# A written order for the matrix engine in the expert stage, and the embedding's weight as one more piece of the expert weights

## The chip, the cores and the metric

The kernel runs on one core of a Trainium2 chip, in one launch. The metric is device time in microseconds (us). Before the change the median of three runs is 1607.17 us (1605.23 to 1608.93). The engines are named as the profile names them: PE is the matrix engine, PEld its weight loads, DVE the vector engine, ACT the scalar engine, POOL the GpSimd engine, and SP the engine that here does little but issue DMAs; SPq is its instruction queue.

## What is computed

Two transformer layers follow each other on 256 tokens of width 1024, all in float32. The first mixes attention and a gated delta rule. The second ends in a mixture of 32 experts, and this is where the change lies:

```python
logits = jnp.dot(xt, w_router) + b_router
top_logit, top_e = lax.top_k(logits, 4)
gate = jax.nn.softmax(top_logit, axis=-1)
...
hh = jnp.dot(xs, w_gu[e]) + b_gu[e]              # 1024 x 2048 per expert
glu, lin = jnp.split(hh, 2, axis=-1)
act = jnp.minimum(glu, 7) * sigmoid(1.702 * glu) * (jnp.clip(lin, -7, 7) + 1.0)
return jnp.dot(act, w_dn[e]) + b_dn[e]           # 1024 x 1024 per expert
...
h = h + moe(rmsnorm_2(h, g_moe), ...)
u = rmsnorm_2(h, g_ple)
h = h + sigmoid(u @ w_ple_gate) * (p @ w_ple_proj)   # the embedding: p is 256 x 256
return rmsnorm_2(h, g_final)
```

The weights of the 32 experts are 12 MiB each, 384 MiB together, and each is read once.

## The kernel before

The expert stage takes most of the time, from about 600 to 1566 us. Each expert has 64 rows for its tokens. Experts go through `run` in 17 units: unit 0 is a single expert, unit 8 is one expert with 128 rows (a "double"), and the other fifteen are pairs of experts.

**The stream of weights.** `pieces` yields the weights in the order in which they are used, cut into pieces of 1 MiB (128 partitions x 2048): the gate/up weights of unit i (16 pieces for a pair), then the down weights of unit i-1 (8 pieces). `load` (line 110) issues a DMA for each from SP's queue into the next of 15 buffers, which are taken in turn and carry the names raw (3 and 4 of them), whi and wlo (4 each). A DMA can start when the piece that lay in its buffer 15 pieces earlier has been used by PE. `refill` in `run` asks for further pieces until all buffers but one are taken; `nxt` hands the next one to the matrix instructions.

**One turn of the loop.** For turn i, `run` writes: the gate/up products of unit i (64 matrix instructions of a pair into four PSUM tiles `ph`); the copies of these into `hs` by ACT and DVE; the down products of unit i-1 (32 instructions into two PSUM tiles of the pool `pm`); and then, in `flush`, what is left over, which this text calls **the rest of the turn**: `gather` for unit i+2 (16 matrix instructions, line 1325), the turning of `hs` and the activation of unit i (`activation`, 16 transposes, line 298, with the additions of the bias on DVE, line 1372), the selection matrix (`scatter_rows`, 2 transposes), and `combine` for unit i-1 (8 matrix instructions, line 1401). The four PSUM tiles of `pm` are shared by the down products and all of the rest.

**How a pair is multiplied.** A pair's two experts each use 64 of PE's 128 columns, so the instruction for one expert and the one for the other can run side by side. `products` writes them alternately:

```python
for j in js:
    ...
    for i in range(2):
        ...
        T.matmul(o[64 * i:64 * i + 64], x(i, c_), w_[:, zz, sl], start=first, stop=last)
```

The order that `run` writes is not the order in which the engines get the instructions: a scheduler of the framework reorders each engine's instructions by its own estimates. In the trace every float32 matrix instruction of the program shows as two records.

**The embedding.** `load_embed` loads `p` and the 1 MiB of `w_ple_proj` in turn 13, by way of the same 15 buffers, and appends to `held`, on which `refill` keeps one buffer fewer filled. `embed` uses them in turn 14 (line 1619) and leaves the product in `pv` for the end of the kernel.

**The end.** After the last down product come the last `combine`, the norm, the product with `w_ple_gate` (lines 152 to 154) and the output.

Of the kernel before, what the change touches and what calls it, by code (L numbers as in the profile page):

```python
# [66 lines left out]
def tile_net(ctx: ExitStack, tc: tile.TileContext, a: dict, dbg=None):  # L67
# [982 lines left out]
    wgu = a["w_gu_2"].rearrange("o e d f -> (o e d) f")  # L1050
    wdn = a["w_dn_2"].rearrange("o e d f -> (o e d) f")

    def pieces(units):

        for i in range(len(units) + 1):
            if i < len(units):
                rs = [p["row"]() for p in units[i]["places"]]
                for k in range(8):
                    for r in rs:
                        yield wgu[bass.ds(r + k * P, P)], 1, 2 * D, "(k p) n -> p k n"  # L1060
            if i:
                rs = [p["row"]() for p in units[i - 1]["places"]]
                for q in range(4):
                    for r in rs:
                        yield wdn[bass.ds(r + q * 2 * P, 2 * P)], 2, D, "(p k) n -> p k n"

    def ahead_or_none(order):
        for src, kc, m, rows in order:
# [16 lines left out]
    with ExitStack() as c3:  # L1085
# [220 lines left out]
        ph = c3.enter_context(tc.tile_pool(name="ph", bufs=4, space=bass.MemoryType.PSUM))  # L1306
        pm = c3.enter_context(tc.tile_pool(name="pm4", bufs=4, space=bass.MemoryType.PSUM))

        def gather(b):

            vs = [v for v, _ in rows_of(b)]
            nb = len(vs)
            dd = wk.tile([P, 2, 2, 64], F32, name="dd", bufs=1)
            for t in range(2):
                for i in range(nb):
                    V.tensor_scalar(dd[:, t, i], iota, vs[i](t), None, ALU.is_equal)
            b["xs"] = wk.tile([P, 8, P], F32, name="xs", bufs=2)
            n = nb * 64
            yield
            for z in range(2):  # L1320
                ps = pm.tile([P, 4, P], F32, name="pm")
                for c_ in range(4):
                    ds_ = slice((4 * z + c_) * P, (4 * z + c_ + 1) * P)
                    for t in range(2):
                        T.matmul(ps[:, c_, :n], ut[t][:, ds_], dd[:, t, :nb], start=t == 0, stop=t == 1)  # L1325
                A.copy(b["xs"][:, 4 * z:4 * z + 4, :n], ps[:, :, :n])
                yield

        def scatter_rows(b):

            dg = wk.tile([P, 2, 2, 64], F32, name="dg", bufs=1)
            rs = rows_of(b)
            for t in range(2):
                for i, (v, g) in enumerate(rs):
                    n = 3 - len(rs)
                    V.tensor_scalar(dg[:, t, i:i + n], bm(iota, n), v(t), g(t), ALU.is_equal, ALU.mult)
            yield
            ps = pm.tile([P, 2, P], F32, name="pm")
            for t in range(2):
                transpose(ps[:, t], dg[:, t].rearrange("p a s -> p (a s)"))  # L1340
            b["oh"] = wk.tile([P, 2, P], F32R, name="ohT", bufs=3)
            b["gs"] = wk.tile([P, 1], F32, name="gs", bufs=3)
            V.tensor_scalar(b["oh"], ps, 0.0, None, ALU.is_gt)
            V.tensor_reduce(b["gs"], ps.rearrange("p t k -> p (t k)"), AX.X, ALU.add)
            yield

        def activation(b, z):
# [4 lines left out]
            if z < n:  # L1352
                gl = []
                for i in range(2):
                    ps = pm.tile([P, m, 64 * n], F32, name="pm")
                    for c_ in range(m):
                        q, k = (z * m + c_) // 2, c_ % 2
                        h = b["hs"][i][:, q * 2 * P + k:(q + 1) * 2 * P:2]
                        if n == 1:

                            T.matmul(ps[:, c_], h, cc("fold"), start=True, stop=True)
                        else:
                            transpose(ps[:, c_], h)
                    gl.append(ps)
                for i in range(2):
                    ps = gl[i]
# [28 lines left out]
        def combine(b, tiles=(0, 1)):  # L1395
            for t in tiles:
                pss = [pm.tile([P, 512], F32, name="pm") for _ in range(2)]
                for nh in range(2):
                    ns = slice(nh * 512, nh * 512 + 512)
                    for i, y in enumerate(b["y"]):  # L1400
                        T.matmul(pss[nh], b["oh"][:, t], y[:, ns], start=i == 0, stop=i == 1)  # L1401
                for nh in range(2):
                    o = hres[:, t, nh * 512:nh * 512 + 512]
                    V.tensor_tensor(o, o, pss[nh], ALU.add)
                yield

        def bias_of(ev):
            br = wk.tile([P, 512], F32, name="sw", bufs=4)[:8, :2 * P]
            SY.dma_start(br, a["b_gu_2"][0].rearrange("e (q f) -> e q f", f=2 * P)[bass.ds(ev, 1)].rearrange("o q f -> (o q) f"))
            ps = pm.tile([P, 2, 8], F32, name="pm")  # L1410
            for k in range(2):
                transpose(ps[:, k], br[:, k::2])
            bi = wk.tile([P, 16], F32, name="bie")
            V.tensor_copy(bi.rearrange("p (q k) -> p k q", k=2), ps)
            return bi

        def run(units, order, ready, more=None, room=None):
# [1 line left out]

            more = more or {}  # L1420
            n = len(units)
            held = []

            def refill():
                while len(ready) < slots() - 1 - len(held):
                    r = ahead_or_none(order)
                    if r is None:
                        return
                    ready.append(r)
# [7 lines left out]
            def products(kd, outs, chunk, x, ws, z, nchunks, js=(0, 1)):  # L1437
# [3 lines left out]
                for j in js:  # L1441
                    o = outs[j]
                    sl = slice(j * 512, j * 512 + 512)
                    if kd == "double":
                        T.matmul(o, x(None, chunk), ws[0][:, z, sl], start=chunk == 0, stop=chunk == nchunks - 1)
                        continue
                    for i in range(2):
                        if kd == "pair":
# [2 lines left out]
                        else:  # L1451
                            c_ = chunk + i
                            w_, zz = (ws[i], z) if len(ws) == 2 else (ws[0], z + i)
                            first, last = c_ < 2, c_ >= nchunks - 2
                        T.matmul(o[64 * i:64 * i + 64], x(i, c_), w_[:, zz, sl], start=first, stop=last)  # L1455

            todo = []

# [8 lines left out]
                todo.clear()  # L1467

            def after(i):
                todo.extend(f(held) for f in more.get(i, ()))  # L1470

            drain(gather(units[0]))
            after(-1)
            if n > 1:
                start(gather(units[1]))
            flush()
            done = []
            for i in range(n + 1):
                if i < n:
# [12 lines left out]
                    b["hs"] = [wk.tile([P, D], F32, name="hs", bufs=2) for _ in range(2)]  # L1492
                    for j in (0, 2, 1, 3):
                        (V.tensor_copy if j // 2 else A.copy)(b["hs"][j // 2][:, j % 2 * 512:j % 2 * 512 + 512], hp[j])  # L1494
                    if i + 2 < n:
                        start(gather(units[i + 2]))
                    sc = scatter_rows(b)
                    next(sc)
                    todo += [activation(b, 0), sc, activation(b, 1)]
# [21 lines left out]
            flush()  # L1521
            return done[0]

        def load_biases(held):
            bdn.extend(wk.tile([P, 512], F32, name="bdn", bufs=2) for _ in range(2))
            for nh in range(2):
                nc.gpsimd.dma_start(bdn[nh][:NE], a["b_dn_2"][0][:, nh * 512:nh * 512 + 512])
            yield

        def biases(held):  # L1530

            gT = wk.tile([P, 2, P], F32, name="gT")
            ps = pm.tile([P, 2, P], F32, name="pm")
            for t in range(2):
                transpose(ps[:NE, t], gate[:, t])
            V.tensor_copy(gT[:NE], ps[:NE])
            yield
            for nh in range(2):
                for t in range(2):
                    ns = slice(nh * 512, nh * 512 + 512)  # L1540
                    ps = pm.tile([P, 512], F32, name="pm")
                    T.matmul(ps, gT[:NE, t], bdn[nh][:NE], start=True, stop=True)
                    V.tensor_tensor(hres[:, t, ns], hres[:, t, ns], ps, ALU.add)
                    yield

        bdn, nov = [], []

        def blocks(held):
            nov.append(nc.values_load(novi[0:1, 0:1], min_val=0, max_val=NJ))
            yield  # L1550

# [40 lines left out]
        big = raw2, RAW2  # L1592
        pv, emb = [], []

        def load_embed(held):

            held.append(1)
            pt = wk.tile([P, 2, 256], F32, name="bdn", bufs=2)
            nc.gpsimd.dma_start(pt, a["p_2"][0, 0].rearrange("(t p) d -> p t d", p=P))
            emb.extend((load(a["w_ple_proj_2"][0], 2, D), pt))  # L1600
            yield

        def embed(held):

            w_, pt = emb
            ps = pm.tile([P, 2, 2, P], F32, name="pm")
            for t in range(2):
                for k in range(2):
                    transpose(ps[:, k, t], pt[:, t, k * P:(k + 1) * P])
            pT = wk.tile([P, 2, S], F32, name="sw", bufs=4)  # L1610
            V.tensor_copy(pT, ps.rearrange("p k t q -> p k (t q)"))
            w_ = w_[:, :2 * D].rearrange("p (k n) -> p k n", k=2)
            yield
            pv.extend(keep.tile([P, D], F32, name="w4") for _ in range(2))
            for t in range(2):
                for nh in range(2):
                    ps = pm.tile([P, 512], F32, name="pm")
                    for k in range(2):
                        T.matmul(ps, pT[:, k, t * P:(t + 1) * P], w_[:, k, nh * 512:nh * 512 + 512], start=k == 0, stop=k == 1)
                    A.copy(pv[t][:, nh * 512:nh * 512 + 512], ps)  # L1620
                    yield
            held.pop()

        first = [lambda held, g=g: g() for g in (chosen, gates, changes, overflow)]
        last = run(units, order, ready, {-1: first, 2: [load_biases], 3: [biases], 4: [blocks], len(units) - 4: [load_embed], len(units) - 3: [embed]})

        if "h3" in dbg:
            SY.dma_start(dbg["h3"].rearrange("(t p) d -> p t d", p=P), hres)
# [88 lines left out]
```

## Time and profile before

| | before |
|---|---|
| runs, median (lowest to highest) | 1607.17 us (1605.23 to 1608.93) |
| profiled execution, its own time | 1613.31 us |
| its span, first to last instruction | 1611.4 us |
| PE busy | 1544.6 us, 96% of the span |
| DVE, ACT busy | 627.6 us, 420.0 us |
| DMA, mean over the span | 301 GB/s, 484.89 MB |
| PE's granted clock, mean | 0.982 of 2.4 GHz |

The profiled execution is 0.4% above the median of the runs. The busy share of PE is a poor guide here: its records are modelled to overlap, and two instructions that run side by side and two that run one behind the other both count as busy. What is to be read instead is at which distance the starts follow each other, which engine waits for which, and how many GB/s the DMA engines move in each stretch.

### The profile page before, as it was taken

The numbers are of one execution on the slowest core, as the hardware profiler recorded it, in microseconds if no ns is written. First come the engines' busy times: TensorE is split into PE (matmuls) and PEld (weight loads), VectorE is DVE, ScalarE is ACT, GpSimd is POOL, SyncE is SP. The second block draws the span as 40 slices with busy tenths as digits, with TensorE's granted clock in tenths as the row PEclk, the third lists the DMA queues.
The fourth block names the chain that finished last, engine by engine and source line by source line (L and its number), as shares of the span: only waits on it lengthen the run. The fifth ranks groups of instructions, "written<-read, shape, count | busy, mean of one in ns | idle before, by whom it ended". The sixth has DMA issues, their size and how long they took to land. (4 is left out here: it accounts for less than half of the span.)

```text
span 1611.4 us, 20470 instructions
## 1 busy us (share of the span) xinstructions
PE 1544.6 (96%) x8162; PEld 959.1 (60%) x8162; DVE 627.6 (39%) x1183; ACT 420.0 (26%) x648; POOL 27.9 (2%) x39
## 2 busy tenths in 40 slices
PE   6999999999889989999999999999999999999996
PEld 5889899999689865444434444444444444443435
DVE  6867765466656642311212321221231132120336
ACT  4544554354447521100101110110110011010124
POOL 0000000000000000000000000000000000000001
PEclk9999999999989979999999999999999999999998
DMA  6443323345434188999999999989999999998992
GB/s 208 157 133 130 105 85 126 106 151 186 138 109 156 53 340 362 420 420 421 420 419 421 420 420 421 421 346 384 398 420 421 421 420 422 419 420 347 422 373 77
DMA packets 99247, 484.89 MB, mean 301 GB/s; under 512 B 10470, under 2 KB 14060, under 8 KB 49996
## 3 DMA queue, kind: packets, MB, share of 16 engines
q1 hardware_dynamic: 99004, 483.14, 75.5%
q8 instruction: 66, 1.08, 0.3%
q0 software_dynamic: 144, 0.39, 0.1%
q14 instruction: 33, 0.27, 0.0%
HBM read 482.46 MB, written 1.05 MB: 300 GB/s over the span
## 5 line engine op out<-in xcount | busy, mean ns | idle before, releaser
L1455 PE MATMUL ph<-raw,xs 128*64 128x512 f32 x928 | 245.1, 599 | 0.0
L1494 DVE COPY hs<-ph 128x512 f32<-128x512 f32 x34 | 23.5, 692 | 443.3 <-PE ph L1455 417.9
L1455 PE MATMUL ph<-wlo,xs 128*64 128x512 f32 x536 | 189.8, 599 | 0.0
L310 DVE TENSOR_TENSOR wlo<-raw,whi 128x2048 fp32r<-128x2048 f32 (+4 forms) x73 | 158.0, 2166 | 79.0 <-ACT whi L309 78.8
L204 PE MATMUL pm<-w,whi 128*128 128x256 f32 x640 | 183.7, 288 | 3.0 <-ACT w L309 2.1
L1455 PE MATMUL ph<-whi,xs 128*64 128x512 f32 x520 | 185.1, 598 | 0.0
L206 PE MATMUL pm<-w,wlo 128*128 128x256 f32 x640 | 180.3, 283 | 2.7 <-DVE wlo L310 2.7
L205 PE MATMUL pm<-w,whi 128*128 128x256 f32 x640 | 180.8, 283 | 2.0 <-DVE w L310 1.9
L1455 PE MATMUL pm<-raw,act 128*64 128x512 f32 x528 | 176.0, 601 | 0.0
L309 ACT CAST whi<-raw 128x2048 fp32r<-128x2048 f32 (+4 forms) x73 | 131.9, 1808 | 157.0 <-PE pm L205 90.5
L1455 PEld LDWEIGHTS ph<-raw,xs 128*64 128x64 f32 x928 | 88.0, 137 | 126.6 <-issue 126.1
L1494 ACT COPY hs<-ph 128x512 f32<-128x512 f32 x34 | 18.5, 588 | 470.7 <-PE ph L1455 443.6
L204 PEld LDWEIGHTS pm<-w,whi 128*128 128x128 f32 x640 | 122.4, 192 | 3.7 <-ACT w L309 2.4
L206 PEld LDWEIGHTS pm<-w,wlo 128*128 128x128 f32 x640 | 122.4, 192 | 3.1 <-DVE wlo L310 3.1
L205 PEld LDWEIGHTS pm<-w,whi 128*128 128x128 f32 x640 | 122.4, 191 | 2.7 <-DVE w L310 2.6
L1455 PEld LDWEIGHTS ph<-wlo,xs 128*64 128x64 f32 x536 | 58.8, 136 | 75.6 <-issue 75.3
L1455 PEld LDWEIGHTS ph<-whi,xs 128*64 128x64 f32 x520 | 57.9, 136 | 74.7 <-issue 74.7
L1455 PEld LDWEIGHTS pm<-raw,act 128*64 128x64 f32 x528 | 51.7, 136 | 81.8 <-issue 76.9
L1455 PE MATMUL pm<-whi,act 128*64 128x512 f32 x240 | 92.1, 601 | 0.0
L1325 PEld LDWEIGHTS pm<-dd,w 128*128 128x128 f32 x544 | 69.0, 204 | 35.7 <-issue 25.2
L1455 PE MATMUL pm<-wlo,act 128*64 128x512 f32 x224 | 87.2, 602 | 0.0
L1325 PE MATMUL pm<-dd,w 128*128 128x128 f32 (+1 forms) x544 | 77.0, 296 | 1.1 <-issue 1.1
(403 smaller groups left out, 1964.9 us busy)
## 6 DMA issues: line engine op xcount, KB each, us to landing
raw<-in_w_gu_dram SPq DMA_DIRECT2D x116, 1024.0 KB, 14.1
wlo<-in_w_gu_dram SPq DMA_DIRECT2D x71, 1024.0 KB, 16.1
whi<-in_w_gu_dram SPq DMA_DIRECT2D x69, 1024.0 KB, 16.7
raw<-in_w_dn_dram SPq DMA_DIRECT2D x66, 1024.0 KB, 14.4
raw<-in_w_in_dram SPq DMA_DIRECT2D x46, 1024.0 KB, 4.9
whi<-in_w_dn_dram SPq DMA_DIRECT2D x32, 1024.0 KB, 15.2
wlo<-in_w_dn_dram SPq DMA_DIRECT2D x30, 1024.0 KB, 15.4
raw<-in_w_branch_a_dram SPq DMA_DIRECT2D x4, 1024.0 KB
```

What stands on the lines that cost most here:

```text
L204: T.matmul(o, hi[:, k, ns], xh[:, k0 + k], start=first, stop=False)
L205: T.matmul(o, hi[:, k, ns], xl[:, k0 + k], start=False, stop=False)
L206: T.matmul(o, lo[:, k, ns], xh[:, k0 + k], start=False, stop=last)
L309: A.copy(hi, src)
L310: (by or V).tensor_tensor(lo, src, hi.bitcast(F32), ALU.subtract)
L1325: T.matmul(ps[:, c_, :n], ut[t][:, ds_], dd[:, t, :nb], start=t == 0, stop=t == 1)
L1455: T.matmul(o[64 * i:64 * i + 64], x(i, c_), w_[:, zz, sl], start=first, stop=last)
L1494: (V.tensor_copy if j // 2 else A.copy)(b["hs"][j // 2][:, j % 2 * 512:j % 2 * 512 + 512], hp[j])
```

## The change

It does four things. Every matrix instruction and transpose of the expert stage goes through `mm` or `turn_`, which ask the framework to keep them in the order in which they are written. The weight of the embedding becomes one more piece of the stream, behind the pieces that turn 12 uses, and `embed` takes it by `nxt` in turn 12; `p` is loaded in turn 6, and `held` goes. The gather of unit 1, which stood ahead of unit 0's gate/up products, now stands behind them with that of unit 2. And `gather`'s one-hot tile `dd` gets a second buffer.

```diff
+    EMB = 12
...
     def pieces(units):
...
+            if i == EMB:
+                yield a["w_ple_proj_2"][0], 2, D, "(k p) n -> p k n"
...
+        def mm(*x_, **y_):
+
+            return tc.keep_in_program_order(T.matmul(*x_, **y_))
+        def turn_(out, in_):
+            k = in_.shape[0]
+            return tc.keep_in_program_order(T.transpose(out, in_, ident[:k, :k]))
...
-            dd = wk.tile([P, 2, 2, 64], F32, name="dd", bufs=1)
+            dd = wk.tile([P, 2, 2, 64], F32, name="dd", bufs=2)
...
-                        T.matmul(o[64 * i:64 * i + 64], x(i, c_), w_[:, zz, sl], start=first, stop=last)
+                        mm(o[64 * i:64 * i + 64], x(i, c_), w_[:, zz, sl], start=first, stop=last)
...
-                while len(ready) < slots() - 1 - len(held):
+                while len(ready) < slots() - 1:
...
             drain(gather(units[0]))
             after(-1)
-            if n > 1:
-                start(gather(units[1]))
             flush()
...
-                    if i + 2 < n:
-                        start(gather(units[i + 2]))
+                    for u_ in units[i + 2:i + 3] if i else units[1:3]:
+                        start(gather(u_))
...
-            emb.extend((load(a["w_ple_proj_2"][0], 2, D), pt))
...
-            w_, pt = emb
+            pt = emb[0]
+            w_ = nxt()
...
-        last = run(units, order, ready, {-1: first, 2: [load_biases], 3: [biases], 4: [blocks], len(units) - 4: [load_embed], len(units) - 3: [embed]})
+        last = run(units, order, ready, {-1: first, 2: [load_biases], 3: [biases], 4: [blocks], 6: [load_embed], EMB - 1: [embed]})
```

**PE, down products of turn 2, before.** The second two of its eight pieces are raw_6274 (first expert) and raw_6276 (second expert); pm_6375 and pm_6376 are the two halves of the result.

```order
L1455 MATMUL pm_6375<-raw_6274,act_6193 64x512
L1455 MATMUL pm_6376<-raw_6274,act_6193 64x512
L1325 MATMUL pm_6441<-dd_6364,w4_5717 128x128
L1325 MATMUL pm_6441<-dd_6364,w4_5715 128x128
L1325 MATMUL pm_6441<-dd_6364,w4_5717 128x128
L298 MATMUL pm_6451<-C0_66,hs_6358 128x128 x4
L1455 MATMUL pm_6375<-raw_6276,act_6193 64x512
L1455 MATMUL pm_6376<-raw_6276,act_6193 64x512
L1455 MATMUL pm_6375<-raw_6274,act_6193 64x512
L1455 MATMUL pm_6375<-raw_6276,act_6193 64x512
L1455 MATMUL pm_6376<-raw_6274,act_6193 64x512
L1455 MATMUL pm_6376<-raw_6276,act_6193 64x512
```

The same two pieces with the change:

```order
L1316 MATMUL pm_6375<-raw_6274,act_6193 64x512
L1316 MATMUL pm_6375<-raw_6276,act_6193 64x512
L1316 MATMUL pm_6376<-raw_6274,act_6193 64x512
L1316 MATMUL pm_6376<-raw_6276,act_6193 64x512
L1316 MATMUL pm_6375<-raw_6274,act_6193 64x512
L1316 MATMUL pm_6375<-raw_6276,act_6193 64x512
L1316 MATMUL pm_6376<-raw_6274,act_6193 64x512
L1316 MATMUL pm_6376<-raw_6276,act_6193 64x512
```

Four of the eight instructions stood with two of the same expert next to each other and other work around them; now first and second expert alternate throughout, and the gather and the transposes stand behind all 32 down products. (All rows now carry line 1316 or 1320, where `mm` and `turn_` stand.) In turn 5, where PE reads a register, the order is still a mixture of the two.

**PE, start of the stage, before**: the end of unit 0's gather (128x64), unit 0's gate/up (ph) and unit 1's gather (128x128).

```order
L1325 MATMUL pm<-dd,w_5715 128x64
L1325 MATMUL pm<-dd,w_5717 128x64
L1455 MATMUL ph<-raw,xs 64x512
L1325 MATMUL pm<-dd,w_5715 128x128
L1325 MATMUL pm<-dd,w_5717 128x128
```

and with the change:

```order
L1316 MATMUL pm<-dd,w_5715 128x64
L1316 MATMUL pm<-dd,w_5717 128x64
L1316 MATMUL ph<-raw,xs 64x512 x25
L1316 MATMUL ph<-whi,xs 64x512
L1316 MATMUL ph<-raw,xs 64x512
```

Unit 1's sixteen gather instructions have moved behind unit 0's 32 gate/up products, where unit 2's sixteen stand too.

**SP, the load of the embedding's weight.** Before, it stands between gate/up pieces of turn 14:

```order
L110 DMA wlo<-in_w_gu_dram 128x2048
L110 ISA
L110 DMA whi<-in_w_gu_dram 128x2048
L110 DMA whi<-in_w_ple_proj_dram 128x2x1024
L110 ISA
L110 DMA wlo<-in_w_gu_dram 128x2048
```

and with the change behind the last down piece of turn 12:

```order
L110 DMA whi<-in_w_dn_dram 128x2048
L110 ISA
L110 DMA wlo<-in_w_dn_dram 128x2048
L110 DMA wlo<-in_w_ple_proj_dram 128x2x1024
L1086 TENSOR_LOAD eidi
L1086 ISA x2
```

The number of DMAs on SP is the same; the one has moved ahead by 62 pieces of the experts.

## Rows read from the trace of the kernel before

**Rows 1.** SP's queue, waits from 540 to 1580 us: for what, us, times, longest.

```profile
SPq L110 <- PE ph L1455: 301.0, 180, 17.1
SPq L110 <- PE pm L1455: 198.6, 80, 8.8
...
SPq L110 <- PE pm L1619: 20.1, 1, 20.1
```

**Rows 2.** Windows: stretch, its length, busy PE, PEld, DVE, ACT, POOL, clock, DMA share, GB/s.

```profile
600.00:640.00 40.00, 40.00 (x215) 21.95 (x216) 14.45 (x59) 6.43 (x10) 0.00 (x0) 0.92 0.89 362
640.00:800.00 160.00, 158.30 (x702) 69.29 (x700) 38.54 (x84) 18.20 (x30) 0.00 (x0) 1.00 1.01 421
...
1060.00:1100.00 40.00, 39.14 (x163) 17.02 (x164) 12.37 (x28) 4.85 (x8) 0.00 (x0) 1.00 0.81 311
...
1140.00:1160.00 20.00, 20.00 (x86) 7.49 (x87) 8.01 (x19) 2.52 (x4) 0.00 (x0) 1.00 0.92 374
...
1480.00:1500.00 20.00, 19.70 (x67) 7.80 (x66) 7.41 (x15) 4.33 (x7) 0.00 (x0) 1.00 0.68 274
```

**Rows 3.** PE's waits, 600 to 1568 us: the longest of the whole answer.

```profile
PE pm L298 <- DVE sw L1372: 6.8, 13, 0.6
```

**Rows 4.** Timeline of PE, turn 2, end: down products among transposes. Start, length, what.

```profile
713.05 1.93 PE L1455 MATMUL pm<-raw,act 128*64 128x512 f32 x4
714.91 0.94 PE L1325 MATMUL pm<-dd,w 128*128 128x128 f32 x6
```

**Rows 5.** Timeline of PE, gate/up products: first and second step of turn 3, first of turn 4.

```profile
734.26 4.13 PE L1455 MATMUL ph<-whi,xs 128*64 128x512 f32 x13
737.81 0.64 PE L1455 MATMUL ph<-wlo,xs 128*64 128x512 f32 x1
...
792.56 3.71 PE L1455 MATMUL ph<-raw,xs 128*64 128x512 f32 x12
```

**Rows 6.** Timeline of PE, rest of turn 9.

```profile
1134.61 3.73 PE L1325 MATMUL pm<-dd,w 128*128 128x128 f32 x32
...
1140.38 0.50 PE L1401 MATMUL pm<-yh,ohT 128*128 128x512 f32 x1
...
1141.05 1.93 PE L1455 MATMUL ph<-wlo,xs 128*64 128x512 f32 x6
...
1143.57 1.08 PE L1455 MATMUL ph<-wlo,xs 128*64 128x512 f32 x4
...
1145.71 1.50 PE L1455 MATMUL ph<-wlo,xs 128*64 128x512 f32 x5
```

**Rows 7.** Timeline of DVE, rest of turn 9.

```profile
1141.24 0.41 DVE L1344 TENSOR_REDUCE gs<-pm 128x1 f32<-128x256 f32 x1
...
1142.17 1.28 DVE L1372 TENSOR_TENSOR sw<-pm,bguT 128x512 f32<-128x512 f32 x2
```

**Rows 8.** Timeline of PE, the embedding's last products.

```profile
1487.35 1.12 PE L1619 MATMUL pm<-whi,sw 128*128 128x512 f32 x2
```

**Rows 9.** Timeline of SP around it.

```profile
1465.89 22.94 SPq L110 DMA_DIRECT2D whi<-in_w_gu_dram  x2
```

**Rows 10.** Timeline of PE, start of the stage.

```profile
600.85 1.97 PE L1455 MATMUL ph<-raw,xs 128*64 128x512 f32 x2
...
608.26 10.52 PE L1455 MATMUL ph<-raw,xs 128*64 128x512 f32 x48
```

**Rows 11.** Timeline of PE, last down products and what follows.

```profile
1565.63 0.59 PE L1455 MATMUL pm<-wlo,act 128*64 128x512 f32 x1
1568.83 0.62 PE L1401 MATMUL pm<-yh,ohT 128*128 128x512 f32 x1 [2.61 <-ACTq L1557]
```

**Rows 12.** Windows ahead of the stage and after it, columns as in rows 2.

```profile
450.00:460.00 10.00, 7.96 (x57) 7.40 (x55) 3.11 (x4) 3.29 (x6) 0.55 (x1) 1.00 0.51 164
...
1569.00:1573.00 4.00, 3.98 (x15) 2.92 (x15) 2.92 (x3) 2.52 (x3) 0.00 (x0) 0.57 0.94 324
```

More of the change, by code (lines that the diff above doesn't have):

```diff
@@ L1324, in gather @@
                     for t in range(2):
-                        T.matmul(ps[:, c_, :n], ut[t][:, ds_], dd[:, t, :nb], start=t == 0, stop=t == 1)
+                        mm(ps[:, c_, :n], ut[t][:, ds_], dd[:, t, :nb], start=t == 0, stop=t == 1)
                 A.copy(b["xs"][:, 4 * z:4 * z + 4, :n], ps[:, :, :n])
@@ L1339, in scatter_rows @@
             for t in range(2):
-                transpose(ps[:, t], dg[:, t].rearrange("p a s -> p (a s)"))
+                turn_(ps[:, t], dg[:, t].rearrange("p a s -> p (a s)"))
             b["oh"] = wk.tile([P, 2, P], F32R, name="ohT", bufs=3)
@@ L1359, in activation @@
                         if n == 1:
-                            T.matmul(ps[:, c_], h, cc("fold"), start=True, stop=True)
+                            mm(ps[:, c_], h, cc("fold"), start=True, stop=True)
                         else:
-                            transpose(ps[:, c_], h)
+                            turn_(ps[:, c_], h)
                     gl.append(ps)
@@ L1400, in combine @@
                     for i, y in enumerate(b["y"]):
-                        T.matmul(pss[nh], b["oh"][:, t], y[:, ns], start=i == 0, stop=i == 1)
+                        mm(pss[nh], b["oh"][:, t], y[:, ns], start=i == 0, stop=i == 1)
                 for nh in range(2):
@@ L1411, in bias_of @@
             for k in range(2):
-                transpose(ps[:, k], br[:, k::2])
+                turn_(ps[:, k], br[:, k::2])
             bi = wk.tile([P, 16], F32, name="bie")
@@ L1421, in run @@
             n = len(units)
-            held = []
             def refill():
-                while len(ready) < slots() - 1 - len(held):
+                while len(ready) < slots() - 1:
                     r = ahead_or_none(order)
@@ L1444, in products @@
                     if kd == "double":
-                        T.matmul(o, x(None, chunk), ws[0][:, z, sl], start=chunk == 0, stop=chunk == nchunks - 1)
+                        mm(o, x(None, chunk), ws[0][:, z, sl], start=chunk == 0, stop=chunk == nchunks - 1)
                         continue
@@ L1469, in after @@
             def after(i):
-                todo.extend(f(held) for f in more.get(i, ()))
+                todo.extend(f(nxt) for f in more.get(i, ()))
             drain(gather(units[0]))
             after(-1)
-            if n > 1:
-                start(gather(units[1]))
             flush()
@@ L1522, in run, with load_biases @@
             return done[0]
-        def load_biases(held):
+        def load_biases(nxt):
             bdn.extend(wk.tile([P, 512], F32, name="bdn", bufs=2) for _ in range(2))
@@ L1528, in load_biases, with biases @@
             yield
-        def biases(held):
+        def biases(nxt):
             gT = wk.tile([P, 2, P], F32, name="gT")
@@ L1534, in biases @@
             for t in range(2):
-                transpose(ps[:NE, t], gate[:, t])
+                turn_(ps[:NE, t], gate[:, t])
             V.tensor_copy(gT[:NE], ps[:NE])
@@ L1541, in biases @@
                     ps = pm.tile([P, 512], F32, name="pm")
-                    T.matmul(ps, gT[:NE, t], bdn[nh][:NE], start=True, stop=True)
+                    mm(ps, gT[:NE, t], bdn[nh][:NE], start=True, stop=True)
                     V.tensor_tensor(hres[:, t, ns], hres[:, t, ns], ps, ALU.add)
@@ L1546, in tile_net, with blocks @@
         bdn, nov = [], []
-        def blocks(held):
+        def blocks(nxt):
             nov.append(nc.values_load(novi[0:1, 0:1], min_val=0, max_val=NJ))
@@ L1593, in tile_net, with load_embed, embed @@
         pv, emb = [], []
[L1595 to L1599, printed above, removed]
-            emb.extend((load(a["w_ple_proj_2"][0], 2, D), pt))
+        def load_embed(nxt):
+            emb.append(wk.tile([P, 2, 256], F32, name="bdn", bufs=2))
+            nc.gpsimd.dma_start(emb[0], a["p_2"][0, 0].rearrange("(t p) d -> p t d", p=P))
             yield
-        def embed(held):
-            w_, pt = emb
+        def embed(nxt):
+            pt = emb[0]
+            w_ = nxt()
             ps = pm.tile([P, 2, 2, P], F32, name="pm")
@@ L1608, in embed @@
                 for k in range(2):
-                    transpose(ps[:, k, t], pt[:, t, k * P:(k + 1) * P])
+                    turn_(ps[:, k, t], pt[:, t, k * P:(k + 1) * P])
             pT = wk.tile([P, 2, S], F32, name="sw", bufs=4)
             V.tensor_copy(pT, ps.rearrange("p k t q -> p k (t q)"))
-            w_ = w_[:, :2 * D].rearrange("p (k n) -> p k n", k=2)
             yield
@@ L1618, in embed @@
                     for k in range(2):
-                        T.matmul(ps, pT[:, k, t * P:(t + 1) * P], w_[:, k, nh * 512:nh * 512 + 512], start=k == 0, stop=k == 1)
+                        mm(ps, pT[:, k, t * P:(t + 1) * P], w_[:, k, nh * 512:nh * 512 + 512], start=k == 0, stop=k == 1)
                     A.copy(pv[t][:, nh * 512:nh * 512 + 512], ps)
                     yield
-            held.pop()
-        first = [lambda held, g=g: g() for g in (chosen, gates, changes, overflow)]
-        last = run(units, order, ready, {-1: first, 2: [load_biases], 3: [biases], 4: [blocks], len(units) - 4: [load_embed], len(units) - 3: [embed]})
+        first = [lambda nxt, g=g: g() for g in (chosen, gates, changes, overflow)]
+        last = run(units, order, ready, {-1: first, 2: [load_biases], 3: [biases], 4: [blocks], 6: [load_embed], EMB - 1: [embed]})
         if "h3" in dbg:
```

## Prediction

> **What bounds the kernel now.** I read the waits first. SP's queue waits for PE and hardly for anything else: 301.0 and 198.6 us for gate/up and down products to give a buffer back [rows 1]. PE waits for the vector engine only, at most 0.6 us at a time, and not once for a weight to land [rows 3]. So the matrix engine sets the pace of the expert stage, and the DMA engines, which look full, are held by it. Next come the windows, for how tight this is. Between its stops the stream moves 421 GB/s, that is 1 MiB in 2.49 us [rows 2], so the 24 pieces of a pair take 59.8 us. PE's turn for a pair is 58.3 us (734.26 to 792.56) [rows 5]. The two are within 3% of each other. PE gains 1.5 us a turn, and with 15 buffers between them that shows as no wait on either side. What is lost is lost in the stops of the stream, where all buffers are full: 40 us at 362 GB/s at the start of the stage, 40 at 311 and 20 at 374 behind unit 8, the double, and 20 at 274 at the embedding [rows 2]. Against 421 they are 5.6, 10.4, 2.2 and 7.0 us, 25.2 us together. Without any stop the last weight would land 25 us sooner.
>
> **The down products in pairs.** Two instructions on the two halves of PE's columns go side by side; two for the same expert can only go one behind the other. A step of gate/up (two pieces, 8 instructions, 16 records) takes 3.55 us [rows 5], or 0.89 us for two instructions side by side. The two that the scheduler put alone between transposes took 1.86 us (713.05 to 714.91) [rows 4]: 0.97 us lost. The order before has five such twos in the 32 down products of a turn (the piece shown has two of them), so 4.8 us. With the change no such two is left. Eight gate/up steps are 28.4 us and four down steps of the same shape 14.2 us.
>
> **The rest of the turn, now in one stretch.** In the written order PE can no longer fill a wait for a PSUM tile with products of the next unit, so waits that were covered show. The trace has one turn in which the scheduler happened to emit just this order, turn 9. From its gather to the next unit's first whole run of products are 11.1 us (1134.61 to 1145.71), of which 1.9 and 1.1 us are products of the next unit used as filling [rows 6]. So the rest costs between 8.1 us (no wait is left) and 11.1 us (every filling was a wait). The tiles that `combine` writes are given back when DVE has read them: after the reduction that ends at 1141.65 and the two additions that end at 1143.45 [rows 7]. Four short products remain then, so I take 9.6 us. What queues behind such a wait is the next unit's gate/up and, behind that, the buffers that SP waits for; with the stream 5 to 7 us a turn longer than PE's work, both have that much to spare.
>
> A pair's turn becomes 28.4 + 14.2 + 9.6 = 52.2 us (at most 53.7). It agrees from the other side: 58.3 - 4.8 = 53.5 us, with some fillings counted twice. Fifteen pairs at 4.6 us less take 69 us from the 965 us between the first gate/up product at 600.85 [rows 10] and the end of the last down product at 1566.2 [rows 11], so PE could be done 69 us sooner. The stream allows 25. The bound changes hands: after a few turns PE waits for each piece to land, and SP finds free buffers.
>
> **The stops, one by one.** Behind the double, PE falls behind the stream by some pieces; if it comes there with nothing in store instead of a full store, 15 buffers take this up. I count both stops, 10.4 + 2.2 us, as gone. At the embedding SP stood from 1465.89 for 22.94 us over two issues [rows 9], 20.1 us of it for the product with the embedding's weight [rows 1], whose last instruction starts at 1487.35 [rows 8]: that weight held one buffer of the ring over a whole turn, and the queue is in order. As a piece that is used in its turn it holds none: 7.0 us. The load and its 16 records stay, and PE's share of them lies in the slack of turn 12. At the start, unit 0's products begin with two records at 600.85, and the others follow at 608.26 behind unit 1's gather [rows 10]; with that gather behind them the first buffers come back up to 7 us sooner. Then two gathers stand ahead of unit 1 and give none back. Of the 5.6 us I take 2.0, with 0 and 5.6 as ends. The load of p and dd's second buffer I put at nothing: POOL's queue has nothing due near it, and DVE is busy 38.5 of 160 us in this stage [rows 2].
>
> **The sum.** 10.4 + 2.2 + 7.0 + 2.0 = 21.6 us. After the last weight PE still owes one step of 3.55 us, as before, and the end of the kernel does not change. The profiled execution took 1613.3 us and would take 1591.7; it stands 6.1 us above the median of 1607.2, so I forecast 1585.6 us for the median. With the ends of the start, and 2 us for a later last step, this case lies between 1580 and 1590.
>
> **Rivals.** *The clock falls because PE waits.* Behind a wait of 2.61 us [rows 11] PE's granted clock is 0.57 in the next window, so mostly 1.2 GHz [rows 12]. With the change PE would wait some 6 us in each turn. For the rival: this. Against it: the waits come in portions, 2 x 2.49 - 3.55 = 1.4 us between steps, and a stretch in which PE was idle for a fifth stayed at 2.4 GHz [rows 12]. It corrects itself too, since a PE at half rate has no waits. A tenth of the 896 us that are left of PE's work at 1.2 GHz adds 90 us and eats the gain; it costs from 44 us (5%) and makes the kernel slower from 69 us (8%). I put the case at 1596 to 1615 us.
> [...]
>
> *PE stays the bound.* If the rest of the turn comes nearer to 14 us, a turn is 56.6 us, the store empties slowly, and the double still stops the stream; the embedding's 7.0 us and some of the double's 12.6 remain as gain: 1594 to 1601 us.
>
> *The written order is slower.* Place: between the last down product of a turn and the first gate/up product of the next, where PE stands in order for `pm` tiles, behind DVE and ACT. The price is the rest of the turn, 17 times. It decides from 58.3 - 42.6 = 15.7 us: at 17 us each of fifteen pairs loses 1.3 us, 20 us, and less the embedding's 7 it is 1620 us. Against it stands turn 9 with 11.1 us at most [rows 6].
>
> That the change doesn't do what it says can be left out: but for turn 5, the listed order is the written one.
>
> **Chances.** Forecast 0.72; PE stays the bound 0.13 (0.12 faster, 0.01 same); clock 0.08 (0.03 faster, 0.02 same, 0.03 slower); slower order 0.07. With 0.2% (3.2 us), about what a measurement of this kernel can tell, as the border: faster 0.87, same 0.03, slower 0.10. The range has to take in the second case: 1579 to 1601 us.
>
> **What would show it.** In the new profile PE's gate/up products should wait for DMA, by about 6 us a turn from unit 6 or so on, and SP's waits for PE should shrink. The windows at the double and in turns 12 and 14 should stand at 420 GB/s. Down products should run at 3.55 us a step, and the turns of pairs should come to 59.8 us late in the stage. I am wrong if PE still has no wait for DMA while the stream stops, if windows of the stage show a clock well under 1, or if the rest of a turn passes 13 us.

## The result, and the profile after

The changed kernel takes 1588.05 us (median of four runs, 1587.23 to 1589.79) against 1608.05 us (four runs, 1605.23 to 1609.07): ratio 0.988, 95% interval 0.9863 to 0.9897, so 20.0 us less where 21.6 were forecast. Its profiled execution took 1589.79 us with a span of 1588.0; that of before lay 5.3 us above its median, so the two spans differ by more than the medians, 23.4 us.

Where the time went is read best between two marks that both traces have: the first product of the router and the last down product. First before, then after, from the timelines of PE:

```profile
583.53 4.80 PE L1181 MATMUL pm<-wr,uT 128*128 128x32 f32 x32
```

```profile
581.58 4.66 PE L1186 MATMUL pm<-wr,uT 128*128 128x32 f32 x32
...
1545.28 0.59 PE L1316 MATMUL pm<-wlo,act 128*64 128x512 f32 x1
```

Between the marks lie 982.7 us before (to 1566.2 [rows 11]) and 964.3 us after: **18.4 us less in the expert stage**. From the last down product to the end of the span were 45.2 us and are 42.1: 3.1 us less. What is left, 1.9 us, lies ahead of the router, where nothing was changed; in the twelve traces of this study the router starts anywhere from 576.9 to 583.5 us. Each kernel has one trace, so a microsecond or two of such differences can be chance.

Windows of after, the columns as in rows 2:

```profile
600.00:640.00 40.00, 40.00 (x230) 20.36 (x228) 10.72 (x42) 6.05 (x9) 0.00 (x0) 0.98 0.96 397
640.00:800.00 160.00, 151.84 (x750) 63.25 (x748) 37.45 (x84) 18.61 (x30) 0.00 (x0) 1.00 1.01 420
1060.00:1100.00 40.00, 38.91 (x200) 16.85 (x196) 11.81 (x27) 6.24 (x10) 0.00 (x0) 1.00 1.01 420
1140.00:1160.00 20.00, 20.00 (x96) 6.62 (x94) 1.38 (x2) 1.17 (x2) 0.00 (x0) 1.00 1.01 420
1160.00:1480.00 320.00, 286.52 (x1354) 117.57 (x1352) 72.16 (x155) 37.43 (x60) 0.00 (x0) 0.99 1.01 421
1480.00:1500.00 20.00, 18.29 (x84) 5.98 (x80) 0.00 (x0) 0.00 (x0) 0.00 (x0) 1.00 1.01 421
```

The stops behind the double and at the embedding are gone (311, 374 and 274 GB/s before [rows 2]). What is left is 2.3 us at the start (40 us at 397 against 421). Now the queue's waits and PE's, first SP's from 540 to 1560 us, then PE's from 598 to 1546:

```profile
SPq L110 <- DMA raw<-in_w_gu_dram: 178.9, 95, 3.5
SPq L110 <- PE ph L1316: 137.4, 71, 14.0
...
SPq L110 <- PE pm L1316: 35.8, 51, 9.8
```

```profile
PE pm L1316 <- DMA raw<-in_w_dn_dram: 23.0, 17, 2.0
PE pm L1316 <- DMA whi<-in_w_dn_dram: 13.6, 10, 2.2
PE pm L1316 <- DMA wlo<-in_w_dn_dram: 11.4, 9, 1.4
PE pm L1316 <- DVE gs L1357: 9.6, 15, 0.7
PE ph L1316 <- DMA raw<-in_w_gu_dram: 6.6, 5, 1.3
PE pm L1316 <- DVE sw L1385: 5.6, 14, 0.4
PE ph L1316 <- DMA wlo<-in_w_gu_dram: 3.3, 3, 1.3
PE ph L1316 <- DMA whi<-in_w_gu_dram: 1.3, 1, 1.3
```

SP's waits for PE's products fell from 499.6 us [rows 1] to 173.2; it now waits for earlier weight transfers to land, 582 us over the six kinds of them, so the stream is full. PE, which never waited for a weight [rows 3], now does so 45 times, 59.2 us in all. The bound has changed hands. PE's own turn shows where nothing has to be waited for, in turn 2 (a row joins records; x64 would be a whole turn's down products):

```profile
669.29 0.65 PE L1316 MATMUL ph<-wlo,xs 128*64 128x512 f32 x2
...
696.80 0.59 PE L1316 MATMUL pm<-wlo,act 128*64 128x512 f32 x1
...
699.82 10.89 PE L1316 MATMUL pm<-raw,act 128*64 128x512 f32 x49
710.64 3.84 PE L1316 MATMUL pm<-dd,w 128*128 128x128 f32 x32
...
717.94 0.47 PE L1316 MATMUL pm<-yh,ohT 128*128 128x512 f32 x1 [0.69 <-DVE gs L1357]
...
719.05 0.50 PE L1316 MATMUL pm<-yh,ohT 128*128 128x512 f32 x1 [0.40 <-DVE sw L1385]
...
720.31 1.94 PE L1316 MATMUL ph<-whi,xs 128*64 128x512 f32 x8
```

The turn lasts 51.0 us (669.29 to 720.31) where it was 58.3 [rows 5], its down products take 13.8 us (696.80 to 710.64), and its rest 9.67 us (710.64 to 720.31), with two short waits for DVE in it.

### The profile page after: what moved, and what is told of

It is laid out like the page before. It is cut to its first block, busy times and chain, and to the rows that moved or that the text cites. A ratio compares the mean times of both kernels' runs of the same rounds, so it can differ in the third digit from the quotient of the medians.

```text
span 1588.0 us, 20479 instructions
## 1 busy us (share of the span) xinstructions
PE 1456.5 (92%) x8162; PEld 902.3 (57%) x8162; DVE 621.5 (39%) x1183; ACT 421.8 (27%) x648; POOL 26.0 (2%) x39
## 5 line engine op out<-in xcount | busy, mean ns | idle before, releaser
L1316 PE MATMUL ph<-whi,xs 128*64 128x512 f32 (+1 forms) x568 | 192.8, 594 | 1.4 <-DMA whi<-in_w_gu_dram 1.3
L1316 PE MATMUL ph<-wlo,xs 128*64 128x512 f32 (+1 forms) x552 | 187.3, 594 | 3.4 <-DMA wlo<-in_w_gu_dram 3.3
L1316 PE MATMUL pm<-raw,act 128*64 128x512 f32 x528 | 150.4, 611 | 23.7 <-DMA raw<-in_w_dn_dram 23.0
L1316 PEld LDWEIGHTS ph<-raw,xs 128*64 128x64 f32 x928 | 74.7, 138 | 141.9 <-issue 127.2
L1503 ACT COPY hs<-ph 128x512 f32<-128x512 f32 x34 | 19.9, 585 | 413.3 <-PE ph L1316 413.3
L1406 DVE SCALAR_TENSOR_TENSOR yl<-pm,gs,yh 128x512 fp32r<-128x512 f32 x34 | 25.4, 749 | 265.1 <-ACT yh L1405 264.4
L1316 PEld LDWEIGHTS ph<-whi,xs 128*64 128x64 f32 (+1 forms) x568 | 62.0, 140 | 83.6 <-issue 76.9
L1316 PE MATMUL pm<-whi,act 128*64 128x512 f32 (+1 forms) x248 | 95.3, 611 | 13.6 <-DMA whi<-in_w_dn_dram 13.6
L1316 PEld LDWEIGHTS ph<-wlo,xs 128*64 128x64 f32 (+1 forms) x552 | 59.3, 140 | 85.0 <-issue 77.4
L1316 PE MATMUL pm<-wlo,act 128*64 128x512 f32 (+1 forms) x248 | 95.0, 597 | 11.4 <-DMA wlo<-in_w_dn_dram 11.4
L1405 ACT ACTIVATE yh<-pm,gs 128x512 fp32r<-128x512 f32 x34 | 23.2, 686 | 282.1 <-PE pm L1316 280.6
## 6 DMA issues: line engine op xcount, KB each, us to landing
wlo<-in_w_gu_dram SPq DMA_DIRECT2D x69, 1024.0 KB, 19.9
```

The lines of the kernel that those rows point to most:

```text
L1316: return tc.keep_in_program_order(T.matmul(*x_, **y_))
L1405: A.activation(yh[:, ns], yp[n_], AF.Copy, scale=b["gs"])
L1406: V.scalar_tensor_tensor(yl[:, ns], yp[n_], b["gs"], yh[:, ns].bitcast(F32), ALU.mult, ALU.subtract)
```

## The experiments

Ten kernels were run. The kernels before and after were not altered otherwise than each diff says. "Stage" is the stretch between the two marks in the profiled execution.

| kernel | median us (runs) | stage us |
|---|---|---|
| before | 1608.05 (4) | 982.7 |
| after | 1588.05 (4) | 964.3 |
| no_pin | 1600.14 (4) | 973.8 |
| embed_held | 1594.13 (4) | 969.9 |
| after_more_pe | 1607.63 (10) | 984.6 |
| before_more_pe | 1683.54 (4) | 1057.3 |
| after_more_stream | 1608.14 (10) | 984.3 |
| before_more_stream | 1613.13 (7) | 988.7 |
| twos_apart | 1589.15 (4) | 963.6 |
| pin_products | 1588.98 (4) | 963.6 |
| gather_first | 1587.23 (4) | 964.3 |
| gather_next | 1585.13 (4) | 961.4 |

**More work for PE, more work for the stream, on both kernels.** These four say who sets the pace. For PE, every gather is done twice:

```diff
-                    for t in range(2):
-                        mm(ps[:, c_, :n], ut[t][:, ds_], dd[:, t, :nb], start=t == 0, stop=t == 1)
+                    for t in range(4):
+                        mm(ps[:, c_, :n], ut[t % 2][:, ds_], dd[:, t % 2, :nb], start=t % 2 == 0, stop=t % 2 == 1)
```

> The changed kernel with the sixteen matrix instructions of every gather done twice, with the same result: about 3.7 us more of PE's work in each pair's turn, 55 to 60 us over the stage. Theory (PE now waits for the stream, a turn of PE's own work is 51 us against 59.8 us of stream): the extra work replaces waits, 1588 to 1592 us, most of the difference at the start. Rival (PE is still the bound over most of the stage): 1635 to 1648 us.

> The kernel before with the same doubled gathers. Theory (there PE's work sets the pace and has no slack): nearly all of the 55 to 60 us appear, 1650 to 1668 us. Rival (the stream was the bound before too, and the stops had another reason): under 1620 us.

For the stream, eight pieces are yielded, loaded and dropped:

```diff
+    EXTRA = (3, 5, 6, 9, 10, 13, 14, 15)
...
+            if len(units) > 1 and i in EXTRA:
+                yield wgu[0:P], 1, 2 * D, "(k p) n -> p k n"
...
                 flush()
+                if n > 1 and i in EXTRA:
+                    nxt()
```

> The changed kernel with eight more pieces of 1 MiB in the stream (a piece of weights loaded once more, in turns 3, 5, 6, 9, 10, 13, 14 and 15, and not used). PE's work is the same. Theory (with the change the stream never stops and sets the end): 8 x 2.49 = 19.9 us more, 1606 to 1609 us. Rival (PE is the bound in part of the stage, and the pieces go into gaps): under 1598 us.

> The kernel before with the same eight pieces of 1 MiB more in the stream, loaded and not used. Theory (before, PE sets the pace and the stream stands still for 25 us of the stage): most of the 19.9 us goes into the stops, 1608 to 1616 us, with the windows behind the double and at the embedding nearer to 421 GB/s. Rival (the stream was as much the bound before as it is after): 1625 to 1629 us.

The extra work of PE is 66.5 us: sixteen gathers at 3.73 us, and 6.8 us for unit 0's, which stands at half the clock (13.88 instead of 7.06 us). Differences of the medians, for the kernel before against its runs beside them (1608.36 and 1607.33 us), for after against 1588.05 us:

| | extra | before | after |
|---|---|---|---|
| PE | 66.5 us | +75.2 us | +19.6 us |
| stream | 19.9 us | +5.8 us | +20.1 us |

Before, all of PE's extra shows and 9 us more, above the 1650 to 1668 us that were expected. The turns of pairs tell of these: most take 63.4 us instead of 58.3 (turn 13, from 1313.68 to 1377.05 us), 5.1 us for 3.73 us of work, and in the compiled order the longer gather leaves one more two of one expert enclosed by full-width instructions on both sides. Most of the stream's extra goes into the stops: the window behind the double rises from 311 to 389 GB/s, that at the embedding from 274 to 420:

```profile
1060.00:1100.00 40.00, 39.15 (x166) 17.11 (x163) 11.62 (x27) 4.85 (x8) 0.00 (x0) 1.00 0.96 389
1480.00:1500.00 20.00, 19.70 (x65) 7.41 (x64) 4.97 (x10) 3.70 (x6) 0.00 (x0) 1.00 1.01 420
```

After, every byte shows. **This is the theory's main point, shown from both sides.** But after_more_pe missed its 1588 to 1592 us: PE's slack is not one sum that can be spent anywhere. Its windows:

```profile
600.00:640.00 40.00, 40.00 (x259) 27.47 (x260) 11.86 (x46) 6.42 (x10) 0.00 (x0) 0.93 0.65 267
1060.00:1120.00 60.00, 58.89 (x296) 26.31 (x295) 13.89 (x30) 7.41 (x12) 0.00 (x0) 1.00 0.95 393
1120.00:1180.00 60.00, 58.90 (x281) 27.62 (x281) 12.51 (x28) 6.24 (x10) 0.00 (x0) 1.00 0.94 388
```

At the start and behind the double all buffers are full; work added there stops the stream, by 14.6, 4.0 and 4.7 us (against 421 GB/s). Less the 2.3 us that the start loses anyway that is 21.0 us, about the 19.6 that were measured; the rest of the 66.5 us disappears in waits.

**The parts of the change.** First the order alone taken away (`mm` and `turn_` as plain calls):

```diff
-            return tc.keep_in_program_order(T.matmul(*x_, **y_))
+            return T.matmul(*x_, **y_)
...
-            return tc.keep_in_program_order(T.transpose(out, in_, ident[:k, :k]))
+            return T.transpose(out, in_, ident[:k, :k])
```

> The changed kernel with the written order taken away again; the embedding as a piece of the stream, the moved gather and the second dd buffer stay. Theory (before, PE's work sets the pace and never waits; the gain comes from the order): PE's work is what it was, so the time is that of before, 1604 to 1609 us, and PE again has no wait for DMA of more than a few us in all. Rival (the stops of the stream are losses of their own, and the embedding's 7 us go with its stop): 1600 to 1602 us.

1600.14 us (ratio 0.9952, interval 0.9935 to 0.9968): the rival's number, but not the rival's reason. PE waits for DMA once, for 1.3 us, so PE still sets the pace and a stop that goes is worth nothing by itself. The stop behind the double is still there, although the moved gather and `dd`'s second buffer are in this kernel too:

```profile
1060.00:1100.00 40.00, 39.15 (x164) 16.87 (x162) 11.40 (x26) 4.85 (x8) 0.00 (x0) 1.00 0.80 315
```

So it is the order that removes that stop. (Whether the order needs the second buffer was not tried.) It is PE's work that shrank here. The turn that now has the embedding, turn 12, of PE's timeline:

```profile
1282.08 7.14 PE L1316 MATMUL pm<-raw,act 128*64 128x512 f32 x32
...
1295.96 7.13 PE L1316 MATMUL pm<-wlo,sw 128*128 128x512 f32 x16
1302.93 3.73 PE L1316 MATMUL pm<-dd,w 128*128 128x128 f32 x32
...
1309.35 0.65 PE L1316 MATMUL ph<-whi,xs 128*64 128x512 f32 x2
```

From 1251.26 to 1309.35 it takes 58.1 us with 7.1 us of embedding in it, no more than the 58.3 us of a turn without: here the scheduler left the down products in one piece and put everything else behind them. Before, it had put the embedding, two or four records at a time, between groups of two and of six down products [rows 8], and that turn, turn 15, took 63.7 us (1434.33 to 1498.03); without the embedding it takes 52.7 in no_pin (1427.61 to 1480.30). (Counted from 0 as all other turns are, the load of the embedding's weight lies in the rest of turn 14 before, and its use in turn 15; the description of the kernel and of the change gives both turns one too low.) So no_pin shows the price of the neighbours, not that of the stop.

Then the embedding as before (`load_embed` in turn 14, `held`, `embed` in turn 15), with the order kept:

```diff
-            if i == EMB:
-                yield a["w_ple_proj_2"][0], 2, D, "(k p) n -> p k n"
...
-                while len(ready) < slots() - 1:
+                while len(ready) < slots() - 1 - len(held):
...
+            held.append(1)
+            emb.extend((load(a["w_ple_proj_2"][0], 2, D), pt))
```

> The changed kernel with the embedding as before: loaded in turn 13, its buffer held over a turn, used in turn 14; the written order stays. Theory (with the order the stream is the bound, so whatever stops it is paid in full): the embedding's stop costs what it cost the stream before, about 7 us: 1592 to 1598 us, with a window near 1480 to 1500 us well under 421 GB/s. Rival (the stored pieces cover the stop, or PE is still the bound): 1587 to 1589 us.

1594.13 us, 6.1 more than after. SP stands for one product, and the stream with it; SP's waits from 1420 to 1500 us, and one window:

```profile
SPq L110 <- PE pm L1314: 19.6, 1, 19.6
```

```profile
1460.00:1480.00 20.00, 18.12 (x74) 8.59 (x72) 10.37 (x21) 6.24 (x10) 0.00 (x0) 1.00 0.59 239
```

That window lacks 8.6 us against 421 GB/s, and 6.1 are paid; where the rest went, the part on the prediction tells. The held buffer, which as far as no_pin's waits show costs nothing by itself while PE is the bound, costs 6 us once the stream is.

**What of the order counts.** In twos_apart everything is pinned, but four times a turn other instructions stand between the two experts' instructions:

```diff
+                            if kd == "pair" and z == 0:
+                                products(kd, yp, 2 * q + z, x, ws, z, 8, only=(0,))
+                                between()
+                                products(kd, yp, 2 * q + z, x, ws, z, 8, only=(1,))
```

(`between` takes the next step of this turn's gather, transposes or selection.)

> The changed kernel, all pinned, but in the down products of a pair the two instructions of the first expert and the two of the second stand apart at four places of a turn, with eight transposes or gather instructions written between them, as the scheduler had it. Theory (two of one expert alone cannot go side by side, 0.97 us a time): 3.9 us more in the down products; as the rest of the turn is then shorter by what its waits were, at most 2 us, turns without waits for DMA (from unit 9 to 10 and 10 to 11: 51 us) become 52.5 to 55 us. The stream has 5 to 8 us to spare in a turn, so the time stays at 1587 to 1591 us. Rival (what counts is that PE has other work to fill waits, not the neighbours): those turns stay at 51 us or become shorter.

Turn 2 of its timeline:

```profile
664.60 0.65 PE L1316 MATMUL ph<-wlo,xs 128*64 128x512 f32 x2
...
692.12 1.88 PE L1316 MATMUL pm<-wlo,act 128*64 128x512 f32 x4
693.92 2.05 PE L1316 MATMUL pm<-dd,w 128*128 128x128 f32 x16
...
701.52 3.71 PE L1316 MATMUL pm<-raw,act 128*64 128x512 f32 x16
...
710.31 3.65 PE L1316 MATMUL pm<-raw,act 128*64 128x512 f32 x12
...
717.67 0.65 PE L1316 MATMUL ph<-whi,xs 128*64 128x512 f32 x2
```

The turn is 53.1 us instead of 51.0, inside the expected 52.5 to 55, but its down products lose 2.5 us (16.3 instead of 13.8) and not 3.9. One expert's first two run alone for 1.8 us ahead of the gather, and the last six instructions (twelve records), four of them the second expert's, take as long as eight, 3.6 us. Between them lie three stretches of eight, four of each expert by the compiled order (here the pieces of both are named raw), and these take 3.6 us as well, where strict alternation takes 3.5. So here it counts whether a stretch between full-width instructions has as many instructions of the one expert as of the other, and their order within it counts little. The order before had twos with full-width instructions on both sides; this edit makes only the first and the last stretch uneven. Some 0.4 us come back: gather and transposes, in pieces, take 0.6 us more, and `combine`, with no wait marked, 1.0 less. The time stays, 1589.15 us, as the stream has room for it. pin_products, with only `products` pinned:

> The changed kernel with only the gate/up and down products pinned; gather, transposes and combine are left to the scheduler, which puts some of them between down products again, so that at some four places a turn one instruction of each expert goes alone (half a two, some 0.5 us each place). Theory (the neighbours in the down products are what the pin is worth; the rest may float): turns without waits for DMA take 51 to 54 us, and the time is 1587 to 1591 us. Rival (the rest must be pinned too, for PE falls behind the scheduler's order of it): 1593 us or more.

Its turn 2 takes 55.0 us (668.15 to 723.18), a little above what was expected, and the kernel 1588.98 us. So the order is worth 3 to 7 us a turn to PE, and how much of that is won doesn't matter here: at 55.0 us a turn the stream still does not stop behind the double (418 GB/s from 1060 to 1100 us), where at 58.3, only 1.5 us under the stream's 59.8, it did (311).

**The start.** gather_first puts unit 1's gather ahead of unit 0's products again; gather_next puts each gather into the turn just before its unit:

```diff
-                    for u_ in units[i + 2:i + 3] if i else units[1:3]:
+                    for u_ in units[i + 1:i + 2]:
```

> The changed kernel with the gather of unit 1 ahead of unit 0's products again, unit 2's behind them, all in the written order; nothing else differs. Theory (at the start all buffers are full, and the stream stops until PE gives some back): the first buffers come back later by a gather of 16 instructions, 3.5 to 7 us, and one gather less stands before unit 1: 1 to 4 us slower, 1589 to 1592 us, seen in the windows from 600 to 640 us alone. Rival (the start has no effect, since PE has slack later): 1587 to 1589 us.

> The changed kernel with each unit's gather in the rest of the turn just before it, instead of two turns ahead: unit 2's sixteen gather instructions no longer stand before unit 1 at the start. Theory (the stream only loses where PE gives no buffer back, and what is left of that is the start, 2.3 us at 600 to 640 us): 1.5 to 2 us gained, 1586 to 1587 us, if PE does not wait for the gathered tile at each turn. Rival (the start is not on the path): 1588 us. Rival (PE waits for the gathered tile in front of each unit): the slack of a turn takes it, 1588 to 1590 us.

gather_first is no slower (1587.23 us, stage 964.3 as in after): the theory missed. Unit 0's products start later, but one gather less stands behind them, and the stream stops as long in sum (392 against 397 GB/s from 600 to 640 us). gather_next has one gather on either side, and the last stop is gone:

```profile
600.00:640.00 40.00, 40.00 (x218) 18.14 (x216) 6.43 (x17) 4.89 (x7) 0.00 (x0) 1.00 1.01 419
```

It takes 1585.13 us (1584.06 to 1586.09; ratio to before 0.9859, interval 0.9841 to 0.9876), 2.9 us less than after, with no run in common: **the fastest of all kernels here**. No window of its stage up to 1500 us shows a stop of the stream any more.

## Why the prediction was right, point by point

- *The bound changes from PE to the stream*: right, and shown by the four kernels with more work. (That SP waits for PE "and hardly for anything else" was read too strongly: the answer behind [rows 1] has 196 us of waits for transfers too, the longest line being the one below. They were not the bound, as PE had no wait for a weight.) That PE set the pace before, although the DMA engines looked full and a pair's turn of stream (59.8 us) was longer than PE's (58.3), is shown by the same four.

```profile
SPq L110 <- DMA raw<-in_w_dn_dram: 59.5, 34, 4.6
```

- *Down products in pairs, the rest in 9.6 us, a turn of 52.2*: 13.8 us against 14.2, 9.67 against 9.6, 51.0 against 52.2.
- *The stops: 10.4 + 2.2 + 7.0 + 2.0 = 21.6 us*: the stage fell by 18.4. At the start the stop went from 5.6 to 2.3 us, more than the 2.0 that were counted, but the reason given (unit 1's gather out of the way) is not the one: with that gather back in front it is 2.8 us. So 22.9 us of stops are gone by the windows, and yet the last weight lands only 19.4 us sooner after the router (978.5 us after it before, 959.1 after). The term that is missing from the sum is the drift of the stream. Each load lands in sixteen parts, whose signals the trace keeps apart. Those of the last weight come from 1560.21 to 1562.00 us before, but from 1532.31 to 1540.66 us after. In after's trace this spread grows from 2 us at 614 us to 8.3; in before's it grows too, and behind each stop it is back at 0.5. The last part lags the mean of the sixteen by 1.3 us before and by 4.6 after, and these 3.3 us are nearly the difference between 22.9 and 19.4. The ten microseconds before it has landed, before, after and in embed_held, whose stop lies 80 us earlier:

```profile
1552.00:1562.00 10.00, 10.00 (x47) 4.32 (x49) 1.41 (x3) 0.00 (x0) 0.00 (x0) 1.00 1.01 411
1530.66:1540.66 10.00, 9.35 (x44) 2.97 (x44) 3.26 (x6) 1.23 (x2) 0.00 (x0) 1.00 0.81 306
1534.70:1544.70 10.00, 9.34 (x44) 3.01 (x44) 3.21 (x6) 1.18 (x2) 0.00 (x0) 1.00 1.01 408
```

So a stop costs less here than it lasts: the embedding's, 7.0 us in the sum and 8.6 in embed_held's window, costs 6.1 where it is taken alone, and embed_held's last weight has a spread of 2.3 us. Why the parts differ in speed was not looked into. Behind the last weight PE takes 5.2 us instead of 4.2 to its last down product (counted as the same 3.55 in the prediction): 19.4 - 1.0 = 18.4.
- *"The end of the kernel does not change"*: wrong, 3.1 us shorter, and that this nearly equals the other error, 3.2, is luck. Before, PE stands in the end for the preparation of the weight of `w_ple_gate` by ACT and DVE (lines 309 and 310), and after it has no such wait (but one of 1.67 us for DVE that before lacks):

```profile
1574.96 0.50 PE L152 MATMUL ph<-whi,raw 128*128 128x512 f32 x1 [1.41 <-ACT raw L309]
1577.71 0.50 PE L154 MATMUL ph<-whi,raw 128*128 128x512 f32 x1 [2.01 <-DVE raw L310]
```

In the traces of all kernels this stretch lies between 42.1 and 45.4 us. In the six that pin every instruction in after's order, the gather's place and number aside, it is 42.1 to 43.0, in the other six 44.5 to 45.4; what of the order decides was not tried.
- *Gate/up products wait for DMA*: the right waits in the wrong place. 48.0 of the 59.2 us fall on the down products. The prediction left out that the stream goes on during the rest of a turn: in 9.7 us about four pieces land. Gate/up lives on these, and gains on the stream 4.98 - 3.5 = 1.5 us a step, so it runs dry near its last steps, and the down products pay.
- *Turns late in the stage 59.8 us*: 60.4 and 59.2 for turns 14 and 15 (starts at 1353.35, 1413.74 and 1472.97). Turn 12, which has the embedding, takes 68.8 and turn 13 then 54.4.
- *The rival of the clock*: no. From 1160 to 1480 us the clock is 0.99, with PE idle for a tenth; two of the short dips told of below lie in this stretch. *The rival of a slower order* decided from a rest of 15.7 us; it is 9.67.

## What to carry to other kernels

Two resources that are both busy over 95% can still have one master: look for who waits for whom, and add work to each in turn if it isn't plain. What the slack of the faster one absorbs depends on where the work falls: full buffers (the start, behind a long unit) have none. The time that a stream loses in stops is a bound of the gain, not the gain: without stops its parts drift apart, and the last one counts. A scheduler that doesn't know which instructions can share the array breaks such pairs up; where the neighbours of an instruction set its price, pin the order, and let the rest float if there is room.

## What the runs showed of the hardware

**The clock falls behind some short waits and comes back.** After's timeline of PE, and windows behind it:

```profile
1006.49 5.34 PE L1316 MATMUL pm<-raw,act 128*64 128x512 f32 x14 [2.00 <-DMA raw<-in_w_dn_dram]
...
1385.88 0.72 PE L1316 MATMUL pm<-whi,act 128*64 128x512 f32 x1 [2.15 <-DMA whi<-in_w_dn_dram]
...
1461.11 0.86 PE L1316 MATMUL pm<-whi,act 128*64 128x512 f32 x1 [2.03 <-DMA whi<-in_w_dn_dram]
```

```profile
1008.00:1010.00 2.00, 2.00 (x8) 0.57 (x5) 0.00 (x0) 0.00 (x0) 0.00 (x0) 0.50 1.00 418
1386.00:1390.00 4.00, 4.00 (x12) 1.20 (x14) 0.00 (x0) 0.00 (x0) 0.00 (x0) 0.57 1.01 420
1390.00:1392.00 2.00, 2.00 (x12) 0.65 (x10) 0.00 (x0) 0.00 (x0) 0.00 (x0) 1.00 1.00 418
1462.00:1464.00 2.00, 2.00 (x6) 0.48 (x5) 0.00 (x0) 0.00 (x0) 0.00 (x0) 0.50 1.02 426
```

Behind these three waits, the longest of the 45 (no other is over 1.43 us), PE is at or near 1.2 GHz for some 4 us and then back at 2.4, while it was working. By an estimate from these windows such a dip costs 2 us of PE's time; the stream went on at 418 to 426 GB/s meanwhile. A fourth dip, 0.50 from 834 to 836 us, has no wait for a transfer ahead of it; it follows the products with the biases. The Trainium skill, "TensorE: Matmul & The Clock Gate", section "HAM oscillation — how this bites in real kernels", tells of a kernel in which the matrix engine starts cold behind each of its waits for a transfer. The waits of that kernel are longer than any here, so no run here tests it; of the 45 shorter waits three end in the low clock.

**Two halves of the columns needn't alternate strictly.** In before's gate/up the compiled order is four instructions of one expert, then four of the other, without anything between; the eight steps take 28.4 us [rows 5], and 27.5 in strict alternation (669.29 to 696.80). So blocks of four cost next to nothing where both experts have as many; a two with full-width instructions on both sides costs 0.97 us [rows 4].
